# Softmax with relative position bias on one core: chunks of seven rows in three buffers, and the bias table read as 132 bytes a partition

## The chip, the core and the metric

The kernel runs on one core of a Trainium2 chip. The metric is the device time of one execution in microseconds (us), the median over the runs. VectorE (DVE), ScalarE (ACT), GpSimd (POOL) and SyncE (SP) are used; TensorE is not.

## What is computed

`logits` has the shape 2 x 8 x 2112 x 2112 in float32 (285 MB), `rel_bias` 8 x 33. Every row of logits gets a bias that depends on the head and on the clipped distance of row and column, and then a softmax along its 2112 columns:

```
rel_clipped = np.clip(pos[:, None] - pos[None, :], -16, 16) + 16
logits = logits + rel_bias[:, rel_clipped][None]
exp = np.exp(logits - logits.max(axis=-1, keepdims=True))
return exp / exp.sum(axis=-1, keepdims=True)
```

## The kernel before

There are 2 x 8 x 2112 = 33,792 rows. Each of the 128 partitions owns 264 consecutive rows (`ROWS`), so a partition lies within one head: 8 partitions (`PB`) make a head, 64 a batch entry. "Row" below means one row in each partition, 128 x 2112 floats or 1056 KB. The kernel walks through the 264 rows in 44 chunks of R = 6 rows, in NBUF = 4 buffers X[0] to X[3] that are loaded, changed in place and stored. Four chunks, 24 rows, are one step of the loops (`STEP`).

**Preparation.** The bias of a row is a window of one long line per partition, M in PSUM: constant at both ends, with the 33 values of the head in between, at a place that depends on the partition. To build M, ScalarE's queue loads the whole table (8 x 33 floats, 1056 bytes) into every partition (L97). Two iotas of GpSimd and a few small VectorE operations (L118 to L128) make masks; L131 multiplies the table by the mask of the partition's own head, and L135 adds over the heads, which leaves the 33 values in rbS. L139 to L155 write M.

**The loops.** Each engine has its own loop, with semaphores between them:

- VectorE: at the top of each step `strip` (L160) copies the window of M that serves the step's 24 rows to F in SBUF. Then for every buffer `add` waits for the load and runs, for each row, one operation (L166) that adds the bias, negates, and takes the minimum (the negated maximum). `scale` waits for ScalarE's exponentials of three rows, takes three reciprocals (L183), multiplies three rows (L187), and again for the other three.
- ScalarE: one activation a row (L175), exp with the row's maximum as its bias and with the row's sum.
- SP issues all loads and stores of the big arrays, in one order written out by hand: store of chunk 0; then, repeated, the store of chunk n + 1 (after its six scales), the wait until the store of chunk n has landed, and the load of chunk n + 4 into the buffer that has come free.

Before the loops SP issues the first loads: chunk 0 as six transfers of one row (L88; the last counts on `ld[0]`, the others on `pre`, for which VectorE waits ahead of its loop), then chunks 1 to 3 as one transfer each. A transfer of six rows reads 50,688 consecutive bytes per partition. At the end, the last chunk is stored in two halves.

`take(engine, semaphore, n)` (L73) waits for a count and subtracts it; it stands in the profile as line L74.

Of the kernel before, what the change touches and what calls it, by code (L numbers as in the profile page):

```python
# [15 lines left out]
def kernel(  # L16
# [18 lines left out]
    N = ROWS // R  # L35
    HALF = R // 2
    assert ROWS % STEP == 0
# [11 lines left out]
    ip = io.tile([P, 3, PB], I32, tag="ip", name="ip")  # L49
    ps = ctx.enter_context(tc.tile_pool(name="ps", bufs=1, space=bass.MemoryType.PSUM))  # L50
    M = ps.tile([P, 4096], FP32, tag="M", name="M")

    def view(t, offset, dims):

        return bass.AP(tensor=t.tensor, offset=t.offset + offset, ap=[[list(t.ap[0])[0], P]] + dims)

    def rows(t, j, n):

        return bass.AP(tensor=t.tensor, offset=t.offset + j * S, ap=[[ROWS * S, P], [1, n * S]])

    with tc.tile_critical(no_gpsimd_drain=True):
        ld = [nc.alloc_semaphore(f"ld{b}") for b in range(NBUF)]
        st = [nc.alloc_semaphore(f"st{b}") for b in range(NBUF)]
# [5 lines left out]
        pre = nc.alloc_semaphore("pre")  # L69
        idx = nc.alloc_semaphore("idx")  # L70
        dve = nc.alloc_semaphore("dve")

        def take(eng, sem, n):  # L73
            eng.wait_ge(sem, n).then_inc(sem, -n)  # L74


        def load(j, b):
            nc.sync.dma_start(out=X[b][:, :], in_=rows(logits, j, R)).then_inc(ld[b], 16)

        def store(j, b, s0=0, n=R):  # L80
            take(nc.sync, scaled, n)
            nc.sync.dma_start(
                out=rows(out, j + s0, n), in_=X[b][:, s0 * S : (s0 + n) * S]
            ).then_inc(st[b], 16)


        for r in range(R):
            nc.sync.dma_start(  # L88
                out=X[0][:, r * S : (r + 1) * S], in_=rows(logits, r, 1)
            ).then_inc(ld[0] if r == R - 1 else pre, 16)  # L90
        for n in range(1, NBUF):
            load(n * R, n)

        rbB = view(F, 0, [[1, H * W]])
        nc.scalar.dma_start(  # L97
            out=rbB,
            in_=bass.AP(tensor=rel_bias.tensor, offset=rel_bias.offset, ap=[[0, P], [1, H * W]]),
        ).then_inc(rb, 16)  # L100
        nc.gpsimd.iota(ip[:, 0], pattern=[[0, PB]], base=0, channel_multiplier=1).then_inc(idx, 1)
        nc.gpsimd.iota(ip[:, 2], pattern=[[1, PB]], base=0, channel_multiplier=0).then_inc(idx, 1)  # L102

        v = nc.vector
        done = [0]
# [8 lines left out]
        SC = H * W  # L114
        mask = [F[:, SC + i * PB : SC + (i + 1) * PB] for i in range(9)]
        dp, dh, eq, hm, gt, le, lt, ra, rz = mask
        v.wait_ge(idx, 2)
        then(v.tensor_scalar(out=ip[:, 1], in0=ip[:, 0], scalar1=3, scalar2=7,  # L118
                             op0=ALU.logical_shift_right, op1=ALU.bitwise_and))
        settle()  # L120
        then(v.tensor_tensor(out=dh, in0=ip[:, 1], in1=ip[:, 2], op=ALU.subtract))  # L121
        then(v.tensor_scalar(out=ip[:, 0], in0=ip[:, 0], scalar1=7, scalar2=None, op0=ALU.bitwise_and))
        settle()
        then(v.tensor_tensor(out=dp, in0=ip[:, 0], in1=ip[:, 2], op=ALU.subtract))  # L124
        then(v.tensor_scalar(out=hm, in0=dh, scalar1=0.0, scalar2=None, op0=ALU.is_equal))
# [5 lines left out]
        then(v.tensor_tensor(  # L131
            out=view(F, 0, [[W, H], [1, W]]), in0=view(F, 0, [[W, H], [1, W]]),
            in1=view(F, SC + 3 * PB, [[1, H], [0, W]]), op=ALU.mult))
# [5 lines left out]
        then(v.tensor_scalar(out=ra, in0=gt, scalar1=low, scalar2=None, op0=ALU.mult))  # L139
        then(v.tensor_scalar(out=rz, in0=gt, scalar1=low, scalar2=None, op0=ALU.mult))  # L140
        then(v.tensor_tensor(  # L141
            out=view(F, 0, [[W, PB], [1, W]]), in0=view(F, SC + 2 * PB, [[1, PB], [0, W]]),
            in1=view(rbS, W - 1, [[0, PB], [-1, W]]), op=ALU.mult))
        settle()
        then(v.scalar_tensor_tensor(out=ra, in0=le, scalar=high, in1=ra, op0=ALU.mult, op1=ALU.add))  # L145
# [2 lines left out]
        U = ROWS - 1 - MR  # L148
        then(v.tensor_tensor(  # L149
            out=view(M, U, [[ROWS, PB], [1, W]]), in0=view(F, 0, [[W, PB], [1, W]]),  # L150
            in1=view(F, SC + 8 * PB, [[1, PB], [0, W]]), op=ALU.add))
        then(v.tensor_copy(out=view(M, U + W, [[ROWS, PB], [1, ROWS - W]]),  # L152
                           in_=view(F, SC + 7 * PB, [[1, PB], [0, ROWS - W]])))
        then(v.tensor_copy(out=M[:, 0:U], in_=low.to_broadcast([P, U])))  # L154
        then(v.tensor_copy(out=M[:, U + PB * ROWS : MW], in_=high.to_broadcast([P, MW - U - PB * ROWS])))  # L155
        settle()

        def strip(j):

            v.tensor_copy(out=F[:, :], in_=M[:, bass.ds(ROWS - STEP - j, FW)]).then_inc(dve, 1)  # L160

        def add(b):
            take(v, ld[b], 16)
            for r in range(b * R, (b + 1) * R):
                x = X[b][:, (r - b * R) * S : (r - b * R + 1) * S]
                v.tensor_tensor_reduce(  # L166
                    out=x, in0=x, in1=F[:, STEP - 1 - r : STEP - 1 - r + S], scale=-1.0, scalar=BIG,
                    op0=ALU.add, op1=ALU.min, accum_out=nmax[:, r : r + 1],
                ).then_inc(added, 1)

        def exps(b):
            for r in range(b * R, (b + 1) * R):
                x = X[b][:, (r - b * R) * S : (r - b * R + 1) * S]
                take(nc.scalar, added, 1)
                nc.scalar.activation(  # L175
                    out=x, in_=x, func=EXP, scale=-1.0, bias=nmax[:, r : r + 1],
                    accum_out=tot[:, r : r + 1],
                ).then_inc(expd, 1)

        def scale(b):  # L180
            for r0 in range(b * R, (b + 1) * R, HALF):
                take(v, expd, HALF)
                v.reciprocal(out=rec[:, r0 : r0 + HALF], in_=tot[:, r0 : r0 + HALF]).then_inc(inv, 1)  # L183
                take(v, inv, 1)
                for r in range(r0, r0 + HALF):
                    x = X[b][:, (r - b * R) * S : (r - b * R + 1) * S]
                    v.tensor_scalar_mul(out=x, in0=x, scalar1=rec[:, r : r + 1]).then_inc(scaled, 1)  # L187
# [9 lines left out]
        with nc.Fori(0, ROWS // STEP, 1, engines=[ENG.Activation]):  # L197
            for b in range(NBUF):
                exps(b)
# [13 lines left out]
        for b in range(NBUF):  # L213
            take(nc.sync, st[b], 32 if b == (N - 1) % NBUF else 16)


# [28 lines left out]
```

## Time and profile before

| | |
|---|---|
| median of 3 runs | 1330.84 us (1330.0 to 1331.05) |
| span of the profiled execution, first to last instruction | 1327.7 us |
| the profiled execution's time beside the median | the span is 3.1 us below it |
| bytes moved | 285.61 MB read, 285.47 MB written |
| VectorE busy | 976.6 us |
| ScalarE busy | 575.2 us |
| the bias load, issue to landing | 6.2 us |
| a load of six rows, issue to landing (median) | 44.6 us |
| a store of six rows, issue to landing (median) | 52.6 us |

Times within the profile count from the first instruction. Busy times exclude waits and the issuing of DMAs. The time from issue to landing of a DMA includes the time that it stands in the queue behind others. In the view of the DMA queues a row has the queue, its packets, their MB, and the time that the packets took as a share of 16 engines; q1 is SP's queue, q10 ScalarE's. A row of a timeline has its start, its length, engine, line and operation, and in brackets the idle time before it and what ended it.

### The profile page before, as it was taken

The page shows a single profiled execution, that of the slowest core. Times are in us where ns is not written, and L with a number is a line of the kernel's source. Part 1 is how long each engine was busy: PE and PEld are TensorE (multiplying, and loading weights), DVE is VectorE, ACT ScalarE, POOL GpSimd, SP SyncE. Part 2 cuts the span into 40 slices and gives each one's busy share as a digit, 9 for nine tenths or more (in the row PEclk, how much of TensorE's full clock was granted, in tenths as well). Part 3 has the DMA queues.
Part 4 walks back from the last instruction along what each step waited for, and adds up shares of the span by engine and source line. Part 5 has one row for each costly group of instructions (what it writes and reads, how often), then busy time and mean ns, then how long its engine had stood idle before and what let it go on. Part 6 is the DMA issues. An engine that isn't in the chain of part 4 may idle for free. (4 is left out here: it accounts for less than half of the span.)

```text
span 1327.7 us, 2454 instructions
## 1 busy us (share of the span) xinstructions
DVE 976.6 (74%) x911; ACT 575.2 (43%) x539; POOL 0.4 (0%) x6
## 2 busy tenths in 40 slices
DVE  6999667777777776687778777677877776687772
ACT  2564333444444343345444333444444343335440
POOL 0000000000000000000000000000000000000000
DMA  9999999999999999999999999999999999999998
GB/s 392 431 428 437 435 420 437 435 434 425 435 437 434 428 435 434 435 429 429 438 438 432 426 438 437 437 425 437 437 437 425 435 440 437 428 432 438 437 426 359
DMA packets 13683, 571.11 MB, mean 430 GB/s; under 512 B 1521, under 2 KB 1649, under 8 KB 1649
## 3 DMA queue, kind: packets, MB, share of 16 engines
q1 hardware_dynamic: 13536, 570.96, 99.6%
q10 hardware_dynamic: 144, 0.14, 0.1%
q14 instruction: 3, 0.02, 0.0%
HBM read 285.61 MB, written 285.47 MB: 430 GB/s over the span
## 5 line engine op out<-in xcount | busy, mean ns | idle before, releaser
L166 DVE CUSTOM_DVE_ANT_0 X<-X,F 128x2112 f32<-128x2112 f32 x264 | 605.2, 2354 | 301.3 <-DVEq L74 301.3
L175 ACT ACTIVATE X<-X,nmax 128x2112 f32<-128x2112 f32 x264 | 541.7, 2052 | 539.3 <-ACTq L74 517.6
L187 DVE TENSOR_SCALAR X<-X,rec 128x2112 f32<-128x2112 f32 x264 | 332.4, 1315 | 13.2
L175 ACT ACT_TABLE_LOAD x11 | 14.1, 1283 | 183.3 <-ACTq L74 183.3
L175 ACT ACTIVATION_READ_ACCUMULATOR X<-X,nmax 128x1 f32 x264 | 49.2, 186 | 0.0
L160 DVE COPY F<-M 128x2135 f32 x11 | 26.1, 2374 | 6.3 <-DVEq L74 6.3
L166 DVE DVE_READ_ACCUMULATOR2_ANT nmax<- 128x1 f32 x264 | 21.7, 82 | 0.0
L183 DVE RECIPROCAL rec<-tot 128x3 f32<-128x3 f32 x88 | 14.9, 170 | 0.0
L131 DVE TENSOR_TENSOR F<-F 128x264 f32<-128x264 f32 x1 | 0.4, 434 | 4.7 <-DMA F<-in_rel_bias_dram 4.7
L152 DVE COPY M<-F 128x1848 f32<-128x1848 f32 x1 | 2.1, 2077 | 0.0
L118 DVE TENSOR_SCALAR ip<-ip 128x8 int32<-128x8 int32 x1 | 0.2, 173 | 1.3 <-POOL ip L102 1.3
L135 DVE TENSOR_REDUCE rbS<-F 128x33 f32<-128x264 f32 x1 | 0.6, 610 | 0.0
L149 DVE TENSOR_TENSOR M<-F 128x264 f32<-128x264 f32 x1 | 0.4, 441 | 0.0
L141 DVE TENSOR_TENSOR F<-F,rbS 128x264 f32<-128x264 f32 x1 | 0.4, 425 | 0.0
L128 DVE TENSOR_SCALAR F<-F 128x8 f32<-128x8 f32 x4 | 0.4, 166 | 0.0
L154 DVE COPY M<-rbS 128x247 f32<-128x247 f32 x1 | 0.4, 408 | 0.0
L139 DVE TENSOR_SCALAR F<-F,rbS 128x8 f32<-128x8 f32 x1 | 0.2, 231 | 0.0
L145 DVE SCALAR_TENSOR_TENSOR F<-F,rbS 128x8 f32<-128x8 f32 x1 | 0.2, 225 | 0.0
L140 DVE TENSOR_SCALAR F<-F,rbS 128x8 f32<-128x8 f32 x1 | 0.2, 222 | 0.0
L146 DVE SCALAR_TENSOR_TENSOR F<-F,rbS 128x8 f32<-128x8 f32 x1 | 0.2, 219 | 0.0
L124 DVE TENSOR_TENSOR F<-ip 128x8 f32<-128x8 int32 x1 | 0.2, 167 | 0.0
L121 DVE TENSOR_TENSOR F<-ip 128x8 f32<-128x8 int32 x1 | 0.2, 166 | 0.0
(9 smaller groups left out, 1.2 us busy)
## 6 DMA issues: line engine op xcount, KB each, us to landing
X<-in_logits_dram SPq DMA_DIRECT2D x43, 6336.0 KB, 44.6
out_dram<-X SPq DMA_DIRECT2D x43, 6336.0 KB, 52.6
X<-in_logits_dram SPq DMA_DIRECT2D x6, 1056.0 KB, 12.1
out_dram<-X SPq DMA_DIRECT2D x2, 3168.0 KB, 21.1
F<-in_rel_bias_dram ACTq DMA_DIRECT2D x1, 132.0 KB, 6.2
```

The costliest lines, as they stand in the source:

```text
L128: then(v.tensor_scalar(out=m, in0=dp, scalar1=0.0, scalar2=None, op0=op))
L131: then(v.tensor_tensor(out=view(F, 0, [[W, H], [1, W]]), in0=view(F, 0, [[W, H], [1, W]]), in1=view(F, SC + 3 * PB, [[1, H], [0, W]]), op= ...
L135: then(v.tensor_reduce(out=rbS[:, :], in_=view(F, 0, [[1, W], [W, H]]), axis=mybir.AxisListType.X, op=ALU.add))
L141: then(v.tensor_tensor(out=view(F, 0, [[W, PB], [1, W]]), in0=view(F, SC + 2 * PB, [[1, PB], [0, W]]), in1=view(rbS, W - 1, [[0, PB], [-1, ...
L149: then(v.tensor_tensor(out=view(M, U, [[ROWS, PB], [1, W]]), in0=view(F, 0, [[W, PB], [1, W]]), in1=view(F, SC + 8 * PB, [[1, PB], [0, W]] ...
L152: then(v.tensor_copy(out=view(M, U + W, [[ROWS, PB], [1, ROWS - W]]), in_=view(F, SC + 7 * PB, [[1, PB], [0, ROWS - W]])))
L154: then(v.tensor_copy(out=M[:, 0:U], in_=low.to_broadcast([P, U])))
L160: v.tensor_copy(out=F[:, :], in_=M[:, bass.ds(ROWS - STEP - j, FW)]).then_inc(dve, 1)
L166: v.tensor_tensor_reduce(out=x, in0=x, in1=F[:, STEP - 1 - r : STEP - 1 - r + S], scale=-1.0, scalar=BIG, op0=ALU.add, op1=ALU.min, accum_ ...
L175: nc.scalar.activation(out=x, in_=x, func=EXP, scale=-1.0, bias=nmax[:, r : r + 1], accum_out=tot[:, r : r + 1],).then_inc(expd, 1)
L183: v.reciprocal(out=rec[:, r0 : r0 + HALF], in_=tot[:, r0 : r0 + HALF]).then_inc(inv, 1)
L187: v.tensor_scalar_mul(out=x, in0=x, scalar1=rec[:, r : r + 1]).then_inc(scaled, 1)
```

## The change

- Chunks have R = 7 rows, in NBUF = 3 buffers; a step is 21 rows. Twelve steps make 252 rows. The last twelve rows go as chunks of 6, 3 and 3 (`LAST`), the middle one in a spare buffer XS of three rows, the last in X[1]. After its loop VectorE makes one more strip for them.
- `scale` works on four rows and then three (`PARTS`).
- Chunk 0 is one transfer, like the others; the semaphore `pre` goes.
- The table is read straight into rbS: two transfers on ScalarE's queue, one for each 64 partitions, in which the source repeats each head's 33 values (132 bytes) for eight partitions. They are issued on ScalarE's queue in program order ahead of everything else. The multiplication and the reduction over the heads go, with the masks for them.
- In the tail SP issues the loads of all three last chunks before the store of the last chunk of seven, and each of them has one store.

The core of the diff:

```
-    R = 6
-    NBUF = 4
+    R = 7
+    NBUF = 3
     STEP = R * NBUF
-    N = ROWS // R
-    HALF = R // 2
+    N = ROWS // STEP * NBUF
+    SPARE = 3
+    LAST = [(N * R, 6, 0, 0), (N * R + 6, 3, NBUF, 6), (N * R + 9, 3, 1, 9)]
+    PARTS = [(0, 4), (4, 3)]
...
+    X.append(io.tile([P, SPARE * S], FP32, tag="XS", name="XS"))
...
-        for r in range(R):
-            nc.sync.dma_start(
-                out=X[0][:, r * S : (r + 1) * S], in_=rows(logits, r, 1)
-            ).then_inc(ld[0] if r == R - 1 else pre, 16)
-        for n in range(1, NBUF):
+        for n in range(B):
+            nc.scalar.dma_start(
+                out=rbS[n * H * PB : (n + 1) * H * PB, :],
+                in_=bass.AP(
+                    tensor=rel_bias.tensor, offset=rel_bias.offset, ap=[[W, H], [0, PB], [1, W]]
+                ),
+            ).then_inc(rb, 16)
+        for n in range(NBUF):
             load(n * R, n)
-        rbB = view(F, 0, [[1, H * W]])
-        nc.scalar.dma_start(
-            out=rbB,
-            in_=bass.AP(tensor=rel_bias.tensor, offset=rel_bias.offset, ap=[[0, P], [1, H * W]]),
-        ).then_inc(rb, 16)
...
-        v.wait_ge(rb, 16)
-        settle()
-        then(v.tensor_tensor(
-            out=view(F, 0, [[W, H], [1, W]]), in0=view(F, 0, [[W, H], [1, W]]),
-            in1=view(F, SC + 3 * PB, [[1, H], [0, W]]), op=ALU.mult))
-        settle()
-        then(v.tensor_reduce(out=rbS[:, :], in_=view(F, 0, [[1, W], [W, H]]),
-                             axis=mybir.AxisListType.X, op=ALU.add))
-        settle()
+        settle()
+        v.wait_ge(rb, 16 * B)
...
         v.sem_inc(dve, -done[0])
-        take(v, pre, 16 * (R - 1))
-        with nc.Fori(0, ROWS - STEP + 1, STEP, engines=[ENG.DVE]) as j:
-            strip(j)
-            take(v, dve, 1)
+        with nc.Fori(0, N * R - STEP + 1, STEP, engines=[ENG.DVE]) as j:
+            strip(bass.ds(ROWS - STEP - j, FW))
             for b in range(NBUF):
-                add(b)
-                scale(b)
+                add(b, R, b * R, STEP - 1)
+                scale(b, PARTS, b * R)
+        strip(slice(0, FW))
+        for j, n, b, r0 in LAST:
+            add(b, n, r0, ROWS - 1 - N * R)
+            scale(b, [(i, 3) for i in range(0, n, 3)], r0)
...
         store(0, 0)
-        with nc.Fori(0, ROWS - 2 * STEP + 1, STEP, engines=[ENG.SP]) as j:
+        with nc.Fori(0, N * R - 2 * STEP + 1, STEP, engines=[ENG.SP]) as j:
             for b in range(NBUF):
                 store(j + (b + 1) * R, (b + 1) % NBUF)
                 take(nc.sync, st[b], 16)
                 load(j + (b + NBUF) * R, b)
-        for n in range(N - NBUF + 1, N - 1):
-            store(n * R, n % NBUF)
-        store((N - 1) * R, (N - 1) % NBUF, 0, HALF)
-        store((N - 1) * R, (N - 1) % NBUF, HALF, R - HALF)
+        store((N - 2) * R, (N - 2) % NBUF)
+        for j, n, b, r0 in LAST:
+            if b < NBUF:
+                take(nc.sync, st[b], 16)
+            load(j, b, n)
+        store((N - 1) * R, (N - 1) % NBUF)
+        for j, n, b, r0 in LAST:
+            store(j, b, n)
```

More of the change, by code (lines that the diff above doesn't have):

```diff
@@ L61 @@
     with tc.tile_critical(no_gpsimd_drain=True):
-        ld = [nc.alloc_semaphore(f"ld{b}") for b in range(NBUF)]
-        st = [nc.alloc_semaphore(f"st{b}") for b in range(NBUF)]
+        ld = [nc.alloc_semaphore(f"ld{b}") for b in range(NBUF + 1)]
+        st = [nc.alloc_semaphore(f"st{b}") for b in range(NBUF + 1)]
         added = nc.alloc_semaphore("added")
@@ L74, in take, with load, store @@
             eng.wait_ge(sem, n).then_inc(sem, -n)
[L77 to L80 removed]
+        def load(j, b, n=R):
+            nc.sync.dma_start(out=X[b][:, 0 : n * S], in_=rows(logits, j, n)).then_inc(ld[b], 16)
+        def store(j, b, n=R):
             take(nc.sync, scaled, n)
[L82 to L100 removed]
+            nc.sync.dma_start(out=rows(out, j, n), in_=X[b][:, 0 : n * S]).then_inc(st[b], 16)
+        for n in range(B):
[6 more added lines that the diff above has]
+        for n in range(NBUF):
+            load(n * R, n)
         nc.gpsimd.iota(ip[:, 0], pattern=[[0, PB]], base=0, channel_multiplier=1).then_inc(idx, 1)
[L102 removed]
+        nc.gpsimd.iota(ip[:, 1], pattern=[[1, PB]], base=0, channel_multiplier=0).then_inc(idx, 1)
         v = nc.vector
@@ L112, in settle @@
             v.wait_ge(dve, done[0])
-        SC = H * W
-        mask = [F[:, SC + i * PB : SC + (i + 1) * PB] for i in range(9)]
-        dp, dh, eq, hm, gt, le, lt, ra, rz = mask
+        SC = PB * W
+        dp, eq, gt, le, lt, ra, rz = [F[:, SC + i * PB : SC + (i + 1) * PB] for i in range(7)]
         v.wait_ge(idx, 2)
-        then(v.tensor_scalar(out=ip[:, 1], in0=ip[:, 0], scalar1=3, scalar2=7,
-                             op0=ALU.logical_shift_right, op1=ALU.bitwise_and))
-        settle()
-        then(v.tensor_tensor(out=dh, in0=ip[:, 1], in1=ip[:, 2], op=ALU.subtract))
         then(v.tensor_scalar(out=ip[:, 0], in0=ip[:, 0], scalar1=7, scalar2=None, op0=ALU.bitwise_and))
         settle()
-        then(v.tensor_tensor(out=dp, in0=ip[:, 0], in1=ip[:, 2], op=ALU.subtract))
-        then(v.tensor_scalar(out=hm, in0=dh, scalar1=0.0, scalar2=None, op0=ALU.is_equal))
+        then(v.tensor_tensor(out=dp, in0=ip[:, 0], in1=ip[:, 1], op=ALU.subtract))
         settle()
@@ L141 @@
         then(v.tensor_tensor(
-            out=view(F, 0, [[W, PB], [1, W]]), in0=view(F, SC + 2 * PB, [[1, PB], [0, W]]),
+            out=view(F, 0, [[W, PB], [1, W]]), in0=view(F, SC + PB, [[1, PB], [0, W]]),
             in1=view(rbS, W - 1, [[0, PB], [-1, W]]), op=ALU.mult))
@@ L156, with strip, add @@
         settle()
-        def strip(j):
-            v.tensor_copy(out=F[:, :], in_=M[:, bass.ds(ROWS - STEP - j, FW)]).then_inc(dve, 1)
-        def add(b):
+        def strip(start):
+            v.tensor_copy(out=F[:, :], in_=M[:, start]).then_inc(dve, 1)
+            take(v, dve, 1)
+        def add(b, n, r0, top):
             take(v, ld[b], 16)
-            for r in range(b * R, (b + 1) * R):
-                x = X[b][:, (r - b * R) * S : (r - b * R + 1) * S]
+            for i in range(n):
+                x = X[b][:, i * S : (i + 1) * S]
@@ L166, in add, with exps @@
                 v.tensor_tensor_reduce(
-                    out=x, in0=x, in1=F[:, STEP - 1 - r : STEP - 1 - r + S], scale=-1.0, scalar=BIG,
-                    op0=ALU.add, op1=ALU.min, accum_out=nmax[:, r : r + 1],
+                    out=x, in0=x, in1=F[:, top - r0 - i : top - r0 - i + S], scale=-1.0, scalar=BIG,
+                    op0=ALU.add, op1=ALU.min, accum_out=nmax[:, r0 + i : r0 + i + 1],
                 ).then_inc(added, 1)
-        def exps(b):
-            for r in range(b * R, (b + 1) * R):
-                x = X[b][:, (r - b * R) * S : (r - b * R + 1) * S]
+        def exps(b, n, r0):
+            for i in range(n):
+                x = X[b][:, i * S : (i + 1) * S]
@@ L174, in exps, with scale @@
                 take(nc.scalar, added, 1)
                 nc.scalar.activation(
-                    out=x, in_=x, func=EXP, scale=-1.0, bias=nmax[:, r : r + 1],
-                    accum_out=tot[:, r : r + 1],
+                    out=x, in_=x, func=EXP, scale=-1.0, bias=nmax[:, r0 + i : r0 + i + 1],
+                    accum_out=tot[:, r0 + i : r0 + i + 1],
                 ).then_inc(expd, 1)
[L180 to L183, printed above, removed]
-                take(v, inv, 1)
-                for r in range(r0, r0 + HALF):
-                    x = X[b][:, (r - b * R) * S : (r - b * R + 1) * S]
-                    v.tensor_scalar_mul(out=x, in0=x, scalar1=rec[:, r : r + 1]).then_inc(scaled, 1)
+        def scale(b, parts, r0):
+            for i0, n in parts:
+                take(v, expd, n)
+                c = slice(r0 + i0, r0 + i0 + n)
+                v.reciprocal(out=rec[:, c], in_=tot[:, c]).then_inc(inv, 1)
+                take(v, inv, 1)
+                for i in range(i0, i0 + n):
+                    x = X[b][:, i * S : (i + 1) * S]
+                    v.tensor_scalar_mul(
+                        out=x, in0=x, scalar1=rec[:, r0 + i : r0 + i + 1]
+                    ).then_inc(scaled, 1)
@@ L208 @@
                 load(j + (b + NBUF) * R, b)
-        for n in range(N - NBUF + 1, N - 1):
-            store(n * R, n % NBUF)
-        store((N - 1) * R, (N - 1) % NBUF, 0, HALF)
-        store((N - 1) * R, (N - 1) % NBUF, HALF, R - HALF)
-        for b in range(NBUF):
-            take(nc.sync, st[b], 32 if b == (N - 1) % NBUF else 16)
+        store((N - 2) * R, (N - 2) % NBUF)
[4 more added lines that the diff above has]
+        store((N - 1) * R, (N - 1) % NBUF)
+        for j, n, b, r0 in LAST:
+            store(j, b, n)
+        for b in range(NBUF + 1):
+            take(nc.sync, st[b], 16)
 _INS = ['logits', 'rel_bias']
```

14 lines of the change are left out of this document (7 added, 7 removed).

## The prediction

> **What bounds the kernel now.** I read the slices of the span first, then the queues and the costliest groups on the same page, then the waits.
>
> ```profile
> span 1327.7 us, 2454 instructions
> DVE 976.6 (74%) x911; ACT 575.2 (43%) x539; POOL 0.4 (0%) x6
> DMA  9999999999999999999999999999999999999998
> GB/s 392 431 428 437 435 420 437 435 434 425 435 437 434 428 435 434 435 429 429 438 438 432 426 438 437 437 425 437 437 437 425 435 440 437 428 432 438 437 426 359
> ...
> q1 hardware_dynamic: 13536, 570.96, 99.6%
> q10 hardware_dynamic: 144, 0.14, 0.1%
> ...
> X<-in_logits_dram SPq DMA_DIRECT2D x43, 6336.0 KB, 44.6
> ...
> F<-in_rel_bias_dram ACTq DMA_DIRECT2D x1, 132.0 KB, 6.2
> ```
>
> The 16 DMA engines are full in every slice: SP's queue q1 keeps them busy for 99.6% of the span, while VectorE has a quarter of it free. The kernel is 571 MB through the DMA engines. Starvation costs at most the missing 0.4%, 5.3 us, which lies at the two ends; nothing in the middle is left to win. VectorE's waits say the same:
>
> ```profile
> DVE X L166 <- DVEq L74: 301.3, 41, 8.8
> ...
> DVE F L131 <- DMA F<-in_rel_bias_dram: 4.7, 1, 4.7
> ```
>
> It waits 301.3 us for loaded chunks, 41 times: loads, not arithmetic, are late. So the change can gain only by moving the same bytes in fewer packets, and can lose wherever it lets the DMA engines run dry. The place for that is the start. Here is its timeline, and DMA rates by stage (columns: length, busy time of VectorE, ScalarE, GpSimd, clock, DMA share, GB/s):
>
> ```profile
> 0.92 0.41 ACTq L97 DMA_DIRECT2D F<-in_rel_bias_dram  x1
> 0.97 3.34 SPq L88 DMA_DIRECT2D X<-in_logits_dram  x6
> ...
> 7.16 0.43 DVE L131 TENSOR_TENSOR F<-F 128x264 f32<-128x264 f32 x1 [4.69 <-DMA F<-in_rel_bias_dram]
> ...
> 8.27 0.23 DVE L139 TENSOR_SCALAR F<-F,rbS 128x8 f32<-128x8 f32 x1
> ...
> 12.06 0.17 DVE L155 COPY M<-rbS 128x16 f32<-128x16 f32 x1
> 18.48 2.38 DVE L160 COPY F<-M 128x2135 f32 x1 [6.26 <-DVEq L74]
> 21.17 2.36 DVE L166 CUSTOM_DVE_ANT_0 X<-X,F 128x2112 f32<-128x2112 f32 x1 [0.31 <-DVEq L74]
> 23.46 0.08 DVE L166 DVE_READ_ACCUMULATOR2_ANT nmax<- 128x1 f32 x1
> ...
> 35.17 3.78 DVE L187 TENSOR_SCALAR X<-X,rec 128x2112 f32<-128x2112 f32 x3
> ```
> ```profile
> 43.07 22.23 SPq L82 DMA_DIRECT2D out_dram<-X  x2
> 81.12 0.36 SPq L78 DMA_DIRECT2D X<-in_logits_dram  x1
> ```
> ```profile
> 2.20:7.20 5.00, 0.31 (x5) 0.00 (x0) 0.00 (x0) 1.00 0.92 270
> 7.20:18.40 11.20, 4.89 (x11) 0.00 (x0) 0.00 (x0) 1.00 1.01 427
> ...
> 60.00:1320.00 1260.00, 929.89 (x855) 548.67 (x514) 0.00 (x0) 1.00 1.00 433
> ```
>
> Today four chunks are loaded ahead: 24 rows of 1.081 MB (1056 KB, one row per partition, 128 partitions) are 25.9 MB, 60 us of DMA. The first store is issued at 43.07 us, the second at 43.07 + 22.23 - 0.34 = 64.96 us, so the queue never empties.
>
> **The change, part by part.**
>
> *The bias load.* Today it is one transfer of 128 rows of 1056 B on ScalarE's queue q10, beside SP's loads on q1. Its 144 packets are 128 rows and 16 completions, nine entries on each of 16 engines, eight partitions to an engine. How the two queues share an engine is the heart of this case. These are packets, MB and share of the two queues, up to 2 us (q10's row), and from 2 to 3, 4 to 5, 5 to 6 and 6 to 7 us:
>
> ```profile
> q10 hardware_dynamic: 3, 0.00, 0.4%
> ```
> ```profile
> q1 hardware_dynamic: 15, 0.13, 85.1%
> q10 hardware_dynamic: 47, 0.05, 25.0%
> ```
> ```profile
> q1 hardware_dynamic: 25, 0.21, 66.2%
> q10 hardware_dynamic: 26, 0.03, 13.3%
> ```
> ```profile
> q1 hardware_dynamic: 34, 0.29, 77.4%
> q10 hardware_dynamic: 33, 0.03, 16.7%
> ```
> ```profile
> q1 hardware_dynamic: 53, 0.37, 90.3%
> q10 hardware_dynamic: 20, 0.01, 3.4%
> ```
>
> Until 3 us q10 has a head start (3 + 47 packets, about three of nine entries per engine). After that the engines serve the queues in turn, one packet each: 25 against 26, 34 against 33. The bias waits one logits packet for each entry of its own. That is cheap now, because SP's first six transfers are single rows, whose packets are 8448 B. At 433 GB/s over 16 engines, 27.1 GB/s each, a turn is 0.31 us.
>
> After the change the first transfer has all seven rows, and by the pattern of the table above (6336 KB in 128 packets of 49.5 KB) its packets are 7 x 8448 = 59,136 B: 2.18 us each. The bias is now two transfers of 64 rows of 132 B. At eight partitions to an engine, a transfer has 8 + 1 entries on 8 engines. No row says whether the second uses the same eight. I take the same, since the instructions differ in the destination alone: 18 entries in one queue. The other answers, nine or ten entries, are a rival below. The Trainium skill (DMA: Bandwidth & Descriptors, section "Why a DMA increments its semaphore by 16 and not by 1") has a transfer use the largest count up to 16 that divides the slowest dimension of both sides, on the lowest-numbered engines; with 64 partitions and 8 heads that is eight, the same eight twice, so by it the sum is the one with 18 entries. The trace of before shows 16 for 128 partitions and nothing of 64.
>
> With two or three entries gone before q1's first packet, the slowest engine has about 16 turns left, each 2.18 us plus 0.05 us of its own: 3.0 + 16 x 2.23 = 38.7, say **39 us** instead of 7. Bounds: 0.31 us a turn if a large packet is cut up for the other queue (3 + 16 x 0.36 = 9 us), and all 18 turns with a slow first packet (44 us). No row shows the two queues together at large packets; I take the large one: 34 beside 33 is a turn by the packet, and nothing in it speaks of the packet's size.
>
> *The table.* VectorE's wait for all 32 counts now holds everything behind it on VectorE: the table, the strip, the first adds; ScalarE waits for the adds, SP's first store for the scales. The masked multiply and the reduction (7.16 to 8.27) go: 1.1 us off this path; the removed mask steps before were hidden by the 4.7 us wait. What remains from L139 to L155 is 12.06 + 0.17 - 8.27 = 3.96 us. The strip to the first add is 21.17 - 18.48 = 2.69 us. Loop entry was hidden by the load wait, so no row has it; between 0 and 1.5 us, taken as 0.5. Landing to start takes about 0.25 us (the last q10 packet is before 7.0, L131 starts at 7.16). The first add starts at a = 39 + 0.25 + 3.96 + 0.5 + 2.69 = **46.4 us**, against 21.17.
>
> *Seven rows instead of six.* A chunk of six took 43.07 - 21.17 = 21.9 us from first add to store, and the next 64.96 - 43.07 = 21.9. One more add is 23.46 - 21.17 = 2.29, one more scale 3.78 / 3 = 1.26: 25.4 us. The split into four and three changes neither. So the first store is issued at 46.4 + 25.4 = 71.8 and the second at 97.2.
>
> *What the DMA engines have to do until then.* Three chunks are loaded ahead, not four: 21 rows, and then the first store's 7: 28 x 1.081 = 30.3 MB, 69.9 us at 433 GB/s, from 2.2 us on. The slow start (270 GB/s for 5 us) adds 5 x (433 - 270) / 433 = 1.9: done at 74.0 us. SP cannot put load 3 in between: it stands behind the second store's wait. That store's first byte moves about 1.2 us after its issue (as the bias did, issued at 0.92 with its first packets just before 2): 98.4. Idle: 98.4 - 74.0 = **24.4 us**, part before the first store, part before the second.
>
> *Afterwards.* With three buffers, between a chunk's landing and the time its store must be ready lie one store and one load, 2 x 17.5 = 34.9 us, against 25.4 of work. The strip (2.4 us every third chunk) fits into VectorE's wait. 9.5 us are to spare, so from the third store on the DMA engines are full again; nothing is given back, since they are the bound.
>
> *Tail.* Today's last store is issued at 1243.89 + 60.13 = 1304.02 and the span ends 23.7 us later, though its own 3 rows take 7.5: it stands in a full queue, and there is no gap to win.
>
> ```profile
> 1243.89 60.13 SPq L82 DMA_DIRECT2D out_dram<-X  x4
> ```
>
> After the change the last 12 rows go as 6, 3 (in the spare) and 3; behind the last load stand stores of 7, 6, 3 and 3 rows, 47 us of DMA. The last chunks are computed in 25.4 + 21.9 + 2 x 13 = 73 us from the landing of the last seven-row chunk, and the DMA engines have 17.5 + 30 + 47 = 94 us of work from there. No gap either: 0.
>
> *Fewer packets.* q1 has 13,536 now. After: 78 transfers of 144 are 11,232, so 144 fewer per engine. Single-row packets (427 GB/s) against six-row ones (433) cost 1.4% of 1.87 us, 26 ns for five more packets, 5 ns each: 0.7 us gained (bounds 0 and 1.5).
>
> *Sum.* 1327.7 - 0.7 + 24.4 = 1351.4 us of span. The profiled execution is 3.1 us shorter by its span than the median of 1330.84, so **1354.5 us**.
>
> **The rivals.**
>
> 1. *The bias comes in time; no change.* If large packets are cut for the other queue, or both transfers slip through before the first large packet, the table is ready by 21.6 us, when chunk 0 lands (2.2 + 1.9 + 17.5). It decides at a bias landing of 14 us (21.6 less 7.4 of table, entry and strip). Then the second store's first byte is at 21.7 + 2 x 25.4 + 1.2 = 73.7, just under 74.0: idle 0, time 1330.84 - 0.7 = 1330.1. For it: q10 is issued first. Against: the head start today let only three of nine entries through, and the second transfer is issued 0.4 us later, behind q1's first. This is also the case in which the change does what it says.
> 2. *Half the turns.* If the second transfer uses the other eight engines, or each uses 16 with 4 + 1 entries, nine or so turns remain: landing at 3 + 9 x 2.23 = 23 us, first add at 30.5, idle 30.5 + 50.8 + 1.2 - 74.0 = 8.5: 1338.6. A result close to it follows if a queue is served in groups of eight packets: the second transfer then waits for one group, 17.5 us, landing at about 21, idle 6.5, 1336.6. Against the group: 34 packets stand beside 33 in one microsecond. The Trainium skill (same page, section "Queues, rings and completion order") says that an engine drains a packet of some 9 to 17 descriptors from one ring before it switches; this would be the case of groups. This trace, at the start, speaks for single turns.
> 3. *Three buffers are too few.* If the engines drift apart, or store receipts come late, by more than the 9.5 us to spare, each of 36 chunks loses something: one microsecond each is 36 us on top, 1390. Against: landing times today follow the queue (44.6 us for a load is three transfers of 15).
>
> **How the numbers follow.** Forecast 0.58, with its own range 1348 to 1361 (14 to 18 turns, the unknown entry); half the turns 0.20; in time 0.16; three buffers too few 0.06. Predicted 1354.5. The range 1335 to 1362 holds the first two cases and leaves out the others. About 0.2%, 1328.2 to 1333.5, is what a measurement of this kernel can tell from no change. Slower by more: 0.84. Within: 0.12, the case in time. Faster: 0.04, that case with the packets' gain at its end and more.
>
> **What would show it.** In the profile after: VectorE's wait for the bias at about 37 us instead of 4.7, the first add near 46, the first and second store issued near 72 and 97, and slices two and three of the DMA row well under 9, all others full. Bias packets one per 2.2 us and engine show the turns; 16 completions between the two transfers show eight engines. Wrong would be: bias landed by 14 us (the step of the turns falls), by 20 to 25 us (the step of the engines), or idle DMA slices in the middle (the step of the buffers).

## The result and the profile after

The changed kernel takes 1364.08 us (six runs, 1356.22 to 1365.58) against 1330.41 of the kernel before (1329.31 to 1331.05): a ratio of 1.0239 estimated over all runs (the two medians give 1.0253), 95% interval 1.0224 to 1.0255. The larger part of the loss, a gap of 27 us at the start, comes by the mechanism that was forecast; 9.6 us more than the forecast were lost, outside its range. The runs differ: two of the six, 1356.22 and 1357.79, lie within the range. The profiled execution is the longest of them, 1365.58 us, with a span of 1363.8 us. The page of the changed kernel:

```profile
span 1363.8 us, 2367 instructions
DVE 977.4 (72%) x896; ACT 575.9 (42%) x540; POOL 0.4 (0%) x6
DMA  9559999999999999999999999999999999999997
GB/s 413 253 250 417 435 425 432 430 430 439 420 442 432 428 434 441 420 442 428 434 437 423 434 427 435 425 432 427 434 427 430 430 416 442 432 430 423 428 428 342
...
q1 hardware_dynamic: 11232, 570.95, 97.5%
q10 hardware_dynamic: 144, 0.02, 0.0%
```

Slices two and three of the DMA row hold the two gaps. The packets of q1 are 11,232, as worked out. But their share is 97.5% of 1363.8, 1330 us, where before it was 99.6% of 1327.7, 1322: fewer packets with the same bytes took some 7 us longer. That is the second thing to explain. First the waits and the start:

```profile
DVE X L149 <- DVEq L76: 313.0, 35, 11.4
...
DVE F L121 <- DMA rbS<-in_rel_bias_dram: 39.8, 1, 39.8
```
```profile
0.92 1.87 ACTq L87 DMA_DIRECT2D rbS<-in_rel_bias_dram  x2
```
```profile
41.90 0.23 DVE L121 TENSOR_SCALAR F<-F,rbS 128x8 f32<-128x8 f32 x1 [39.81 <-DMA rbS<-in_rel_bias_dram]
...
46.32 2.38 DVE L142 COPY F<-M 128x2132 f32 x1 [0.47 <-DVEq L175]
49.02 2.36 DVE L149 CUSTOM_DVE_ANT_0 X<-X,F 128x2112 f32<-128x2112 f32 x1 [0.32 <-DVEq L76]
```
```profile
74.43 25.72 SPq L84 DMA_DIRECT2D out_dram<-X  x2
100.41 0.35 SPq L80 DMA_DIRECT2D X<-in_logits_dram  x1
```

The bias of 8.2 KB a transfer is there at 41.9 us instead of 7.2; the first add starts at 49.0, the stores are issued at 74.43 and 74.43 + 25.72 - 0.34 = 99.81, and load 3 only behind the second of them. How the two queues shared the engines, from 6 to 10 us (q10; before 6 us it has no packet) and from 10 to 20 us:

```profile
q10 hardware_dynamic: 16, 0.00, 0.3%
```
```profile
q1 hardware_dynamic: 64, 3.78, 87.3%
q10 hardware_dynamic: 32, 0.00, 0.3%
```

q1 runs on 16 engines: 4 packets each in 10 us. q10's 32 packets are 4 each if they lie on 8 engines: one for one. And 144 packets are 128 rows and 16 completions, 8 for each transfer. That is the step of the prediction on engines and turns, in large packets.

By stage (columns as before: length, VectorE, ScalarE, GpSimd, clock, DMA share, GB/s), the changed kernel and then the kernel before:

```profile
56.00:75.50 19.50, 19.20 (x18) 11.28 (x12) 0.00 (x0) 1.00 0.12 49
75.50:93.00 17.50, 17.35 (x18) 15.04 (x14) 0.00 (x0) 1.00 0.88 378
93.00:101.00 8.00, 7.85 (x8) 0.00 (x0) 0.00 (x0) 1.00 0.28 118
101.00:140.00 39.00, 27.33 (x25) 15.04 (x14) 0.00 (x0) 1.00 1.00 411
140.00:600.00 460.00, 334.79 (x304) 199.15 (x187) 0.00 (x0) 1.00 1.00 432
600.00:1300.00 700.00, 513.96 (x468) 305.11 (x286) 0.00 (x0) 1.00 1.00 429
```
```profile
140.00:600.00 460.00, 337.46 (x309) 198.96 (x187) 0.00 (x0) 1.00 1.00 433
600.00:1300.00 700.00, 517.74 (x479) 310.32 (x292) 0.00 (x0) 1.00 1.00 433
```

Right behind the gaps, from 101 to 140 us, the changed kernel moves 411 GB/s (the kernel before 432 in the same stretch); from 140 to 600 us the two move nearly the same. From 600 us on the DMA engines of the changed kernel are as full as before (share 1.00) and carry 429 GB/s instead of 433: the packets themselves take longer, "stretched" below. 700 x (433 - 429) / 433 is 6.5 us.

### The profile page after: what moved, and what is told of

It is laid out like the page before. It is cut to its first block, busy times and chain, and to the rows that moved or that the text cites. A ratio compares the mean times of both kernels' runs of the same rounds, so it can differ in the third digit from the quotient of the medians.

```text
span 1363.8 us, 2367 instructions
## 1 busy us (share of the span) xinstructions
DVE 977.4 (72%) x896; ACT 575.9 (42%) x540; POOL 0.4 (0%) x6
## 3 DMA queue, kind: packets, MB, share of 16 engines
q1 hardware_dynamic: 11232, 570.95, 97.5%
## 5 line engine op out<-in xcount | busy, mean ns | idle before, releaser
L149 DVE CUSTOM_DVE_ANT_0 X<-X,F 128x2112 f32<-128x2112 f32 x261 | 597.9, 2354 | 313.0 <-DVEq L76 313.0
L158 ACT ACTIVATE X<-X,nmax 128x2112 f32<-128x2112 f32 x261 | 535.4, 2052 | 491.9 <-ACTq L76 471.3
L171 DVE TENSOR_SCALAR X<-X,rec 128x2112 f32<-128x2112 f32 x261 | 327.6, 1315 | 11.2
L142 DVE COPY F<-M 128x2132 f32 (+1 forms) x13 | 30.8, 2369 | 0.5 <-DVEq L175 0.5
L121 DVE TENSOR_SCALAR F<-F,rbS 128x8 f32<-128x8 f32 x1 | 0.2, 230 | 39.8 <-DMA rbS<-in_rel_bias_dram 39.8
L167 DVE RECIPROCAL rec<-tot 128x4 f32<-128x4 f32 (+1 forms) x76 | 13.0, 171 | 4.8 <-DVEq L76 4.8
L158 ACT ACTIVATE XS<-XS,nmax 128x2112 f32<-128x2112 f32 x3 | 6.2, 2055 | 8.4 <-ACTq L76 8.2
L149 DVE CUSTOM_DVE_ANT_0 XS<-XS,F 128x2112 f32<-128x2112 f32 x3 | 6.9, 2352 | 0.0
L171 DVE TENSOR_SCALAR XS<-XS,rec 128x2112 f32<-128x2112 f32 x3 | 3.8, 1313 | 0.1
## 6 DMA issues: line engine op xcount, KB each, us to landing
X<-in_logits_dram SPq DMA_DIRECT2D x36, 7392.0 KB, 44.3
out_dram<-XS SPq DMA_DIRECT2D x1, 3168.0 KB, 19.9
out_dram<-X SPq DMA_DIRECT2D x1, 3168.0 KB, 14.1
```

Of the source, the lines that this page charges most:

```text
L142: v.tensor_copy(out=F[:, :], in_=M[:, start]).then_inc(dve, 1)
L149: v.tensor_tensor_reduce(out=x, in0=x, in1=F[:, top - r0 - i : top - r0 - i + S], scale=-1.0, scalar=BIG, op0=ALU.add, op1=ALU.min, accum_ ...
L158: nc.scalar.activation(out=x, in_=x, func=EXP, scale=-1.0, bias=nmax[:, r0 + i : r0 + i + 1], accum_out=tot[:, r0 + i : r0 + i + 1],).then ...
L167: v.reciprocal(out=rec[:, c], in_=tot[:, c]).then_inc(inv, 1)
L171: v.tensor_scalar_mul(out=x, in0=x, scalar1=rec[:, r0 + i : r0 + i + 1]).then_inc(scaled, 1)
```

## The experiments

Two theories to test. **Turns**: the bias transfers wait one large logits packet for each entry of their own. **Slack**: the stretching of the middle belongs to a ring in which a store becomes ready shortly before its turn. Rivals stood for each: the small rows are slow in themselves; the gap at the start, the size of the packets, or VectorE's work beside the transfers stretches the packets. Ratios below are to the kernel before, run beside each on the same chip.

### e1: chunk 0 in small transfers again

```
-        for n in range(NBUF):
+        for r in range(4):
+            nc.sync.dma_start(out=X[0][:, r * S : (r + 1) * S], in_=rows(logits, r, 1)).then_inc(pre, 16)
+        nc.sync.dma_start(out=X[0][:, 4 * S : R * S], in_=rows(logits, 4, R - 4)).then_inc(ld[0], 16)
+        for n in range(1, NBUF):
             load(n * R, n)
...
         v.sem_inc(dve, -done[0])
+        take(v, pre, 64)
```

> The changed kernel, but chunk 0 is loaded as four transfers of one row and one of three rows; the bias load stays on ScalarE's queue as it is. Theory (turns): the bias waits one logits packet for each of its own 18 entries on an engine, so with 8448-byte packets at the start (0.31 us a turn) it lands near 9 us instead of 41, the first add is near 22 us, both gaps before the first two stores go, and 27 us of the 34 us loss come back: 1337 us. Rival (the small rows of 132 bytes are slow in themselves): landing still near 40, 1364. A second question is the 10 us beside the gaps, in which packets of the middle take longer than their usual 2.18 us: if the idle gap at the start causes it (the engines start the first store in step), it goes too, and the time is 1327 to 1330.

Measured: 1340.51 us (1340.33 to 1340.96), ratio 1.0077 (1.006 to 1.0093). Its VectorE timeline:

```profile
10.91 0.23 DVE L129 TENSOR_SCALAR F<-F,rbS 128x8 f32<-128x8 f32 x1 [8.81 <-DMA rbS<-in_rel_bias_dram]
15.55 2.38 DVE L150 COPY F<-M 128x2132 f32 x1 [0.69 <-DVEq L77]
22.81 2.36 DVE L157 CUSTOM_DVE_ANT_0 X<-X,F 128x2112 f32<-128x2112 f32 x1 [4.88 <-DVEq L77]
```

The bias transfers are untouched, and the bias is there at 10.9 us instead of 41.9, only because the packets beside them are small. 1364.08 - 1340.51 = 23.6 us come back. The 132-byte rows are not slow in themselves. The stretching did not go with the gap: 1340, not 1327 to 1330.

### e2: the kernel before with chunk 0 as one transfer

```
-        for r in range(R):
-            nc.sync.dma_start(
-                out=X[0][:, r * S : (r + 1) * S], in_=rows(logits, r, 1)
-            ).then_inc(ld[0] if r == R - 1 else pre, 16)
-        for n in range(1, NBUF):
+        for n in range(NBUF):
             load(n * R, n)
...
-        take(v, pre, 16 * (R - 1))
```

> The kernel before, with one part of the change alone: chunk 0 as one transfer of six rows (50,688-byte packets). Theory (turns): the old bias load has 9 entries on each of 16 engines, some two gone before the first logits packet, so about seven turns of 1.9 us: landing between 16 and 21 us instead of 7, first add between 24 and 29. The time stays at 1330 (within 2 us), because 24 rows are loaded ahead (62 us of work for the DMA engines) and the first store is issued near 50. Rival (the new form of the bias load is what is slow, not the packets beside it): landing at 7, first add near 20.

Measured: 1330.08 us (1329.14 to 1331.71), ratio 0.9999 (0.9989 to 1.0008). The queues between 6 and 10 us, and VectorE:

```profile
q1 hardware_dynamic: 32, 1.62, 101.0%
q10 hardware_dynamic: 32, 0.03, 3.7%
```
```profile
16.25 0.43 DVE L127 TENSOR_TENSOR F<-F 128x264 f32<-128x264 f32 x1 [13.79 <-DMA F<-in_rel_bias_dram]
...
24.48 2.36 DVE L162 CUSTOM_DVE_ANT_0 X<-X,F 128x2112 f32<-128x2112 f32 x1 [0.32 <-DVEq L74]
```

32 packets against 32, on all 16 engines: the old bias load pays the turns too, and lands at 16 us instead of 7. It costs nothing, because 24 rows are loaded ahead. So the one transfer is harmless beside a bias load of 9 entries with 24 rows loaded ahead; whether 18 entries or 21 rows alone would make it harmful was not tried.

### e3: the bias in front, on SP's queue

```
-            nc.scalar.dma_start(
+            nc.sync.dma_start(
                 out=rbS[n * H * PB : (n + 1) * H * PB, :],
```

> The changed kernel with one edit: both bias transfers are issued on SP's queue ahead of the first load, so that they stand in the same queue in front of it. Theory (turns): landing between 3 and 5 us, first add when chunk 0 has landed, near 22 to 23, no gap before the first stores: 1337 to 1338 us if the stretched packets of the middle belong to seven-row chunks in three buffers, 1328 to 1330 if they come from the idle gap at the start. Rival (132-byte rows slow in themselves): landing near 40 and 1364 again.

Measured: 1337.88 us (ten runs, 1330.84 to 1341.48), ratio 1.0049 (1.003 to 1.0068).

```profile
3.91 0.23 DVE L121 TENSOR_SCALAR F<-F,rbS 128x8 f32<-128x8 f32 x1 [1.81 <-DMA rbS<-in_rel_bias_dram]
...
22.80 2.36 DVE L149 CUSTOM_DVE_ANT_0 X<-X,F 128x2112 f32<-128x2112 f32 x1 [12.09 <-DVEq L76]
```

In one queue there are no turns: the bias is there at 3.9 us, 26.2 us come back, and the packets of chunk 0 are as large as in the changed kernel. Together with e1 that settles the gap. What is left over the kernel before, 7.6 us, goes with the stretching; its runs differ by 10 us among themselves. Two of the ten took 1330.8 us, as long as the kernel before, so the stretching does not come in every execution; the profile is of one that took 1340.27.

### e4: six rows in three buffers

Edit to e3: `R = 6`, `PARTS = [(0, 3), (3, 3)]`; the rest follows.

> The kernel of e3 with chunks of six rows in three buffers (50,688-byte packets as in the kernel before; the tail is the same). Theory (slack): the packets of the middle are stretched because with three buffers a store becomes ready only 8 us before its turn (two transfers of 14.95 us less 21.9 us of work), so that engines that have run ahead are held: the stretching stays, the time is not below that of e3, 1337 to 1342. Rival (size): the 59,136-byte packets cause it: with 50,688 bytes the q1 packets take 1322 us over 16 engines as before, and the time is 1329 to 1331.

Measured: 1347.44 us (1340.83 to 1348.78), ratio 1.0118 (1.0087 to 1.015): slower than e3, and packets are as small as before. Its stages and, below it, those of e3:

```profile
140.00:600.00 460.00, 338.94 (x312) 202.05 (x190) 0.00 (x0) 1.00 1.00 431
600.00:1300.00 700.00, 513.64 (x470) 302.02 (x285) 0.00 (x0) 1.00 1.00 427
```
```profile
140.00:600.00 460.00, 334.17 (x303) 198.41 (x186) 0.00 (x0) 1.00 1.00 432
600.00:1300.00 700.00, 516.24 (x467) 304.29 (x285) 0.00 (x0) 1.00 1.00 429
```

With 8 us ahead instead of 9.5 the rate is lower still. The size of the packets is out as the cause.

### e5: stores ready earlier, by leaving out work

```
-                    x = X[b][:, i * S : (i + 1) * S]
+                    x = X[b][:, i * S : i * S + 256]
                     v.tensor_scalar_mul(
```

> The kernel of e3 (seven rows, three buffers, bias first on SP's queue), but each row's final multiplication covers its first 256 columns alone and the other columns are left unscaled: a chunk's work falls by about 7 us, from 25.4 to some 18, and a store is ready some 17 us before its turn instead of 9.5. Theory (slack): the engines may run 7 us further apart, the stretching of packets in the middle ends, q1 takes about 1319 us over 16 engines instead of 1329, and the time is 1328 to 1331. Rival (three buffers or seven-row packets as such): stretching and time stay at those of e3, 1337 to 1340.

Measured: 1330.9 us (1329.2 to 1333.12), ratio 1.0007 (0.9998 to 1.0017), against 1337.88 of e3.

```profile
140.00:600.00 460.00, 247.43 (x303) 198.41 (x186) 0.00 (x0) 1.00 1.00 433
600.00:1300.00 700.00, 394.79 (x480) 315.00 (x295) 0.00 (x0) 1.00 1.00 434
```

Seven rows, three buffers, one transfer for chunk 0, and no stretching after 600 us. The profile is of the quickest of the ten runs. And VectorE also does less beside the transfers, so the run left one rival; e12 took it up.

### e12: stores as early as in e5, VectorE as busy as before

Edit to e5, in VectorE's loop behind `scale`; the final multiplication still covers 256 columns alone:

```
                 scale(b, PARTS, b * R)
+                for _ in range(R):
+                    v.tensor_scalar_mul(
+                        out=F[:, 0:1856], in0=F[:, 0:1856], scalar1=1.0
+                    ).then_inc(dve, 1)
+                    take(v, dve, 1)
```

> The kernel of e5 (final multiplication over 256 columns alone, so stores are ready some 17 us before their turn), but VectorE makes up for the work that is left out: after each chunk's multiplications it runs seven multiplications by 1 over 1856 columns of F in place, while it would wait for the next load. VectorE's busy time is again near 980 us, the stores are as early as in e5. Theory (slack): 1328 to 1333 us as in e5, no stretching after 600 us. Rival (VectorE's work beside the transfers stretches the packets when there are three buffers): 1336 to 1340 as in e3, DMA rate after 600 us near 429 GB/s.

Measured: 1331.52 us (1330.45 to 1332.85), ratio 1.0009 (1.0 to 1.0019).

```profile
DVE 1007.6 (76%) x1148; ACT 575.8 (43%) x540; POOL 0.4 (0%) x6
```
```profile
600.00:1300.00 700.00, 541.65 (x612) 311.85 (x293) 0.00 (x0) 1.00 1.00 434
```

VectorE is busier than in any other run, and the rate is 434, in a profile of the slowest of the ten runs: its work is not the cause. What e5 and e12 share is the moment at which the stores, and the loads that SP issues behind them, are ready. (The added work writes F and not the buffers that the transfers use; whether that matters was not tried.)

### e6: the new table read with six rows in four buffers

Edit to e3: `R = 6`, `NBUF = 4`, chunks and stores at the end as before, no spare.

> Chunks of six rows in four buffers as before, with the table read of the change (132 bytes a partition) issued on SP's queue ahead of the first load, and chunk 0 as one transfer; tail as before. Theory (turns and slack): no gap and almost no stretching, 1329 to 1331 us, the same as before within 0.2%: the new way of reading the table does no harm where it doesn't share engines with large packets. Rival (one of the other edits costs something of its own): above 1333.

Measured: 1332.49 us (1330.16 to 1335.07), ratio 1.0013 (1.0003 to 1.0022); 434 GB/s after 600 us:

```profile
600.00:1300.00 700.00, 516.61 (x477) 311.13 (x292) 0.00 (x0) 1.00 1.00 434
```

No stretching with four buffers. The time is up by about 2 us on the median, at the edge of what the runs tell apart; not followed up. The table read gains nothing where the first load is what is waited for.

### e7: stores on ScalarE's queue

```
         def store(j, b, n=R):
-            take(nc.sync, scaled, n)
-            nc.sync.dma_start(out=rows(out, j, n), in_=X[b][:, 0 : n * S]).then_inc(st[b], 16)
+            take(nc.scalar, scaled, n)
+            nc.scalar.dma_start(out=rows(out, j, n), in_=X[b][:, 0 : n * S]).then_inc(st[b], 16)
...
             for b in range(NBUF):
+                store(j + b * R, b)
+                c = (b + 1) % NBUF
+                exps(c, R, c * R)
```

> The kernel of e3, but the stores are issued on ScalarE's queue, each ahead of the exponentials of the next chunk, and SP issues loads alone, as soon as the buffer's store has landed instead of behind the next chunk's store. Theory (slack): what runs short in the ring is the work that stands ready for an engine that is ahead; with a load in the queue early, no engine is held, the stretching goes, 1327 to 1331 us. Rival (two queues that take turns by packet cost more than one): 1340 or more, and longer landing times for both kinds.

Measured: 1350.58 us (1343.75 to 1353.15), ratio 1.0135 (1.0106 to 1.0163).

```profile
X<-in_logits_dram SPq DMA_DIRECT2D x36, 7392.0 KB, 39.9
out_dram<-X ACTq DMA_DIRECT2D x36, 7392.0 KB, 40.4
```

Loads and stores now share the engines from two queues. A store takes 40.4 us to land instead of 27.0 in the changed kernel, a load 39.9 instead of 44.3, and the rate is 428 GB/s from 140 us on already. My expectation failed, and the run says little about slack: it changes the order of all transfers.

### e8 to e11: each store in two parts

```
+        def store2(j, b):
+            for i, n in PARTS:
+                take(nc.sync, scaled, n)
+                nc.sync.dma_start(
+                    out=rows(out, j + i, n), in_=X[b][:, i * S : (i + n) * S]
+                ).then_inc(st[b], 16)
...
```

e8 is e3 with this, e9 is e4 with it; e10 and e11 are e8 again, for more profiles.

> The kernel of e3 with all its work, but each chunk of seven rows is stored in two transfers, the first four rows as soon as they are scaled and then three: the first bytes of a store stand ready 4 us sooner, some 13.5 us before their turn instead of 9.5. Theory (slack): stretching falls well below the 11 us of e3, the time is 1329 to 1334. Rival (e5 was faster because VectorE does a quarter less work beside the transfers, not for the slack): stretching and time stay, 1336 to 1340.

> The kernel of e4 (six rows, three buffers) with each store in two transfers of three rows, the first some 4 us sooner: 12 us ahead of its turn instead of 8. Theory (slack): stretching falls from 17 us to a few, time 1331 to 1338 instead of 1347. Rival (work beside the transfers, or six rows in three buffers as such): 1345 to 1349.

> The kernel of e8 once more, for a profile: its profiled execution had a span of 1330.9 us with 5 us of stretching, while the median of its timed runs was 1340. Theory (slack, with a limit): an execution near 1340 has its q1 time longer by 5 to 9 us and the engines' completions of one transfer spread over 11 us or more, as far as the ring lets the leaders run ahead. Rival (the spread does not matter, the packets are stretched by something else that differs from run to run): the completions lie within 8 us, below what the ring allows, and the stretching goes on to the end all the same.

> The same kernel a third time, as the executions differ: the same two readings as for e10.

Measured: e8 1340.26 us (five runs, 1332.62 to 1342.15), ratio 1.0079 (1.0062 to 1.0096); e9 1344.3 (1343.77 to 1346.45), ratio 1.0107 (1.009 to 1.0124); e10 1338.64 and e11 1335.26, one run each. By the time, the expectation failed: no gain over e3, and for six rows 3 us less than e4 with intervals that overlap. The profiles of e8, e10 and e9, from 600 us on:

```profile
600.00:1300.00 700.00, 521.35 (x473) 309.70 (x290) 0.00 (x0) 1.00 1.00 433
```
```profile
600.00:1300.00 700.00, 518.77 (x469) 306.63 (x287) 0.00 (x0) 1.00 1.00 431
```
```profile
600.00:1300.00 700.00, 516.56 (x473) 301.84 (x283) 0.00 (x0) 1.00 1.00 428
```

For seven rows the stretching is milder (433 and 431 against 429 in e3; e11 has 433), but e8's profile is of the quickest execution of its kernel, and the splitting adds packets: 16,560 on q1 instead of 11,376. For six rows it is almost unchanged.

The packet records of these traces show one thing more, that the spread of the engines goes with the stretching. Completions of one transfer in the changed kernel, from 154 to 156 us and from 607 to 610 us:

```profile
DMA packets 32, 0.95 MB, mean 473 GB/s; under 512 B 16, under 2 KB 16, under 8 KB 16
```
```profile
DMA packets 26, 1.01 MB, mean 335 GB/s; under 512 B 9, under 2 KB 9, under 8 KB 9
```

Packets under 512 B are the completions, 16 to a transfer, one from each engine. Early, all 16 lie within 2 us; later, 3 us hold only 9. The engines drift apart. The first and the last completion of a load tell when the first and the last engine are through with it and come to the store behind it. The table has how long after that store's issue this was, for the stores issued from 900 to 1210 us (medians, with the range of the first engine; where stores are split, worked out from the packets of the loads, which have a size of their own):

| kernel | first engine, us | last engine, us | GB/s from 600 us on |
|---|---|---|---|
| changed kernel | 1.6 (0.8 to 1.9) | 9.0 | 429 |
| e1 | 1.4 (1.1 to 1.8) | 9.3 | 428 |
| e3 | 1.4 (1.1 to 1.7) | 9.3 | 429 |
| e4 | 1.5 (0.7 to 1.7) | 7.8 | 427 |
| e9 | 1.7 (0.7 to 1.9) | 11.7 | 428 |
| e10 | 2.5 (2.0 to 3.2) | 12.9 | 431 |
| e11 | 4.3 (4.3 to 4.4) | 12.9 | 433 |
| e8 | 7.1 (7.1 to 7.2) | 12.9 | 433 |
| e12 | 6.8 (6.6 to 6.9) | 14.5 | 434 |
| e5 | 9.5 (9.5 to 9.6) | 14.5 | 434 |

The times for the last engine are near the slack of the arithmetic: 9.5 us for seven rows and 8 for six, 13.5 and 12 with the store split, but 14.5 instead of 17 in e5 and e12. The first engine has much less. In every kernel at 427 to 429 GB/s it comes to a store that was issued less than 2 us before; in every kernel at 433 or 434 it comes 4 us or more after the issue. So the spread grows until the leading engines reach the store that is issued late, and the packets stay stretched there: from 700 to 1300 us they took, per engine, 6.8 us more than their usual length in e3, 0.3 in e5 and 0.5 in e12. e9 fits in. An earlier first part lets its engines drift further, 10 us instead of 6 to 7 in e4, until they meet the store again. e10's first reading, a spread of 11 us, came true at the end of its trace, still growing, with q1's time 2 us above e8's and not 5 to 9. Shown is that late stores hold the leaders and that the stretching goes with it. Why the packets take longer then is not shown; that the held engines start the store together is a guess. Nor is it known what lets one execution of a kernel stop drifting at 5.8 us (e8) and another go on to 11 (e10).

## Why the prediction was wrong, point by point

- **What bounds the kernel**: right. Every run that keeps the DMA engines full and unstretched comes out between 1330 and 1333, whatever the chunks.
- **Turns, packet size, eight engines, the same eight twice**: right. One for one in the rows, 18 entries on 8 engines.
- **The head start**: wrong. Two or three entries were to be gone before q1's first packet; q10 has none before 6 us, and q1 is two packets ahead on each engine. Issuing the two transfers took 1.23 and 0.61 us, where the old one took 0.41, and their first packet comes late whatever runs beside it: in e1 at 5.07 us, when q1 has moved 120 small packets. The last packet of q10 is at 41.30 us, 2.3 us later than the forecast landing, and the first add is 2.6 us later than forecast (49.02 against 46.4). That about 16 turns were waited for all the same ((41.3 - 7) / 2.18 = 15.7) is luck: all 18 entries stood behind q1, but where q1 had only completions to move (16 of its 96 packets from 20 to 30 us, 16 of 80 from 30 to 40), an entry got through without waiting for a large packet.
- **Table, loop entry, strip**: right. 3.96 us from L121 to L137 were counted; the loop entry is 0.47 against 0.5 assumed.
- **Seven rows**: right. 74.43 - 49.02 = 25.4 us.
- **Gap**: 24.4 predicted. The second store is 99.81 - 97.2 = 2.6 us late, so 27.0; e1 and e3 gave back 23.6 and 26.2.
- **Afterwards**: this is the step that failed. "From the third store on the DMA engines are full again" is true, and I took that as full speed. The sum put the middle at 433 GB/s and 0.7 us below before; it ran at 429 from 600 us on. The profiled span is 0.3 us below the median, not 3.1, so that the 9.6 us by the medians are 12.4 by the spans (1363.8 against 1351.4). Of these 2.6 are the gap and 9.8 are here: 39 x (433 - 411) / 433 = 2.0 right behind the gaps, 460 x 1 / 433 = 1.1 up to 600 us and 6.5 from there to 1300; the rest is within the rounding of these rates. The 9.5 us to spare were compared with zero. They hold for the last engine (9.0 measured); the first one, ahead of it by the spread, has 1.6 left. The spread could have been read in the trace of before, where from 600 us on the 16 completions of a transfer lie 5.6 us apart; the landing times held against the third rival do not show it. That rival named the drift, with 1 us a chunk; 9.8 / 36 is 0.27.
- **Fewer packets**: not visible. q1's share is above what it was before, because of the stretching.
- **Tail**: right to about a microsecond. The last two stores land 19.9 and 14.1 us after issue, their own transfer being 7.5; by the packet records the DMA engines are idle for 6.1 of the last 30 us, before for 4.9.
- **Rivals**: "in time" and "half the turns" did not happen; the rule of a group of 9 to 17 descriptors (the Trainium skill, DMA: Bandwidth & Descriptors, "Queues, rings and completion order") has not shown here either: 34 packets beside 33 at 8448 bytes, 32 beside 32 at 50,688, and 64 on 16 engines beside 32 on 8 at 59,136.

No version of these is measurably faster than the kernel before: the best with the whole computation are e2 and e6, 1330.08 and 1332.49.

## What to carry to other kernels

A small transfer that something waits for does not get through quickly because its queue is free: beside large packets on the same engines it pays one of them for each of its own entries. Put it on the same queue in front, or keep the first packets small. And "the DMA engines are full" is not "at full rate": the engines here drifted 5 to 11 us apart, so count the slack of a ring from the first engine and not from the last. Here a store issued less than 2 us before the first engine came to it went with a loss of 4 to 6 GB/s, one issued 4 us or more before it with no loss.

## What the runs showed of the hardware that was not expected

- The two bias transfers whose source has three dimensions took 1.23 and 0.61 us to issue on ScalarE's queue (0.77 and 0.61 in front on SP's), against 0.41 for the plain one; on ScalarE's queue they reached the engines behind a load that was issued later.
- Packets that usually take 2.18 us take longer around changes of transfer (in e3 from 700 us on, 97% of the extra time lies in packets that run while the engines are on two different transfers); in three-buffer rings with late stores that is worth 4 to 6 GB/s of 433, with the DMA row at 9 throughout.
- The 16 engines drift apart in every kernel here. In the kernel before the spread of one transfer's completions grows from 1 us to 5.6 at 600 us and stays there; in the rings with late stores it grows until the first engine meets the store.
- Loads and stores on two queues, issued in another order for it, cost 12.7 us over the same kernel on one queue (1350.58 against 1337.88).
